# Hi parts from ScalarE, lo parts from VectorE, in the output and up projections of a two-layer transformer

## The chip, the cores and the metric

The kernel runs on one core of one Trainium2 chip. The metric is the time of one execution on the device in microseconds (us); a smaller number is better. The engines are called PE (TensorE, the matrix engine), DVE (VectorE), ACT (ScalarE), POOL (GpSimd) and SP (SyncE, which issues nearly all DMAs). Each works off its own instructions strictly in order, and waits where an operand is not there yet.

## The reference, cut to what matters

Two layers over 1024 latent tokens of width 1024, with 256 context tokens in front. Layer 0 mixes tokens by a gated MLP beside a neighbourhood attention, layer 1 by grouped-query attention. Then each layer does the same, here for the latent tokens (in layer 0 the context tokens take the same path):

```python
y = mixed @ w_out                                   # output projection, 1024 x 1024
h = h + gt_m * rms_norm(y, g_post_m)
f = modulate(h, g_pre_f, sh_f, sc_f) @ w_up         # up projection, 1024 x 5632
f = conv3(f); a, g = split(f)
h = h + gt_f * rms_norm((silu(g) * a) @ w_down, g_post_f)
```

All of it is float32.

## The kernel before

A float32 product is made of three faster matmuls. `split` (L113) cuts an operand into a hi part, which is a cast to the format fp32r, and a lo part, which is the operand less its hi part. PE then adds up hi x hi, hi x lo and lo x hi. So each operand costs one CAST and one TENSOR_TENSOR, and `split` is told on which engine each is done: "s" for ACT, "v" for DVE, "p" for POOL. Weights come in by `wload` and `part`, always with the hi part (`whi`) on ACT and the lo part (`wlo`) on DVE.

`mlp()` is the function that runs for each layer from the output projection on. The **output projection** has three groups of token tiles: half A of the latent tokens, in layer 0 the context tokens (C), and half B. Each group is multiplied first with one half of the weight's columns and then with the other. The token operands of B and C (`opB`, `opC`) are read back from memory, eight tiles each of 128x512 (B) or 128x256 (C), and are split in `out_load` (L405) while A is being multiplied. In the trace these tiles are called `xb` (parts) and `xd` (what was read); the matmuls are those of `gemm_tok`, L319 to L321, which write `by`.

The **up projection** forms a 1024x1024 by 1024x5632 product by a scheme of seven products in place of eight (after Strassen and Winograd). The activations are cut into blocks, and the seven moving operands are B11, B21, T2, T1, T3, B22 and T4; T1 to T4 are differences of blocks, formed by the subtractions at L938. Four 128x512 tiles make one operand. In the trace the parts of T2 are `xb24` to `xb31`, those of T1 `xb0` to `xb7`, those of T3 `xb8` to `xb15`, and those of B22 and T4 are `xd` tiles, with `xe` for the very last lo part. For each of the 22 column blocks `run` takes two weight blocks, forms two pairs of weight sums on POOL (`sw`, L460 and L461, then L463 and L464), splits them, multiplies (`product`, L500 to L502) and adds the seven results together (`z`, L479 on DVE and POOL). PE's order in a column begins with B11, B21, then T2, T1, T3, B22, T4. POOL's second pair of sums goes into the same tile as the first, so it waits until the first pair's `wlo` on DVE has been formed.

In the kernel before, `out_load` casts on DVE, and the lo parts of even tiles come from DVE, those of odd tiles from POOL. T2 is split on DVE altogether. T1, T3, B22 and T4 are cast on DVE, with lo parts again from DVE (even) and POOL (odd). A framework sets the order of the instructions of each engine beforehand, by a model of their durations and of what they depend on; the order in which the program creates them decides only between those that could run at once. `issue_after(x)`, which the change uses, makes it place instructions behind the instruction x.

Of the kernel before, what the change touches and what calls it, by code (L numbers as in the profile page):

```python
# [9 lines left out]
F32 = mybir.dt.float32  # L10
F32R = mybir.dt.float32r
AF = mybir.ActivationFunctionType
ALU = mybir.AluOpType
# [5 lines left out]
T = 1024  # L19
C = 256  # L20
# [8 lines left out]
HF = 512  # L29
# [26 lines left out]
class Net:  # L56
# [55 lines left out]

    def split(self, hi, lo, src, hi_eng="s", lo_eng="v"):  # L113
        nc = self.nc
        if hi_eng == "s":
            nc.scalar.copy(hi, src)  # L116
        else:
            nc.vector.tensor_copy(hi, src)  # L118
        if lo_eng == "p":
            nc.gpsimd.tensor_tensor(lo, src, hi.bitcast(F32), op=ALU.subtract)  # L120
        else:
            nc.vector.tensor_tensor(lo, src, hi.bitcast(F32), op=ALU.subtract)  # L122

    def wload(self, src, shape):
        raw = self.t(self.wp, [P, 1024], "wraw", 3)
# [279 lines left out]
    def out_load(self, xm, k, yT, c0, n, raw, eng):  # L405
        nc = self.nc
        nc.sync.dma_start(raw[:, :n], yT[k][:, c0:c0 + n])
        if eng == "sp":
            self.split(xm[0][k][:, :n], xm[1][k][:, :n], raw[:, :n], "s", "p")
        elif eng == "pp":  # L410
            nc.gpsimd.tensor_scalar(xm[0][k][:, :n], raw[:, :n], 1.0, 1.0, op0=ALU.mult, op1=ALU.mult)
            nc.gpsimd.tensor_tensor(xm[1][k][:, :n], raw[:, :n], xm[0][k][:, :n].bitcast(F32), op=ALU.subtract)
        else:
            self.split(xm[0][k][:, :n], xm[1][k][:, :n], raw[:, :n], "v", eng)
# [461 lines left out]
    def mlp(self, xa, opA, l, ctx, yT, w_out, src, mid, dst, ahead=None, after=None):  # L876


        nc, tc = self.nc, self.tc
# [5 lines left out]
        with ExitStack() as e0:  # L885
# [3 lines left out]
            with self.banks(out=4, turn=2):  # L889
              with self.banks(junk=1, tmp=1):  # L890
                with ExitStack() as e1:
                  xb2 = pool("xd", e1)
                  E = lambda dt=F32: self.t(xb2, [P, HF], "xd", 16, dt)
                  with ExitStack() as e2:
# [10 lines left out]
                      opB = [[B(8 * i + k) for k in range(KD)] for i in range(2)]  # L905
                      opC = None
                      for k in range(KD):
                          self.out_load(opB, k, yT, HF, HF, E(), "p" if k % 2 else "v")
                      if ctx:
                          opC = [halves(B(16 + k)) for k in range(KD)]  # L910
                          opC = [[x[:, i] for x in opC] for i in range(2)]
                          for k in range(KD):
                              self.out_load(opC, k, yT, T, C, E(), "p" if k % 2 else "v")

                      def ops(t):
                          o = opC if t >= 8 else opB if t >= 4 else opA
# [3 lines left out]
                      op = self.out_proj(ops, w_out, [[0, 1, 2, 3]] + ([[8, 9]] if ctx else []) + [[4, 5, 6, 7]], gates, src, mid)  # L920
# [15 lines left out]
                      st = {v: [E() for _ in range(4)] for v in ("T1", "T3", "B22", "T4")}  # L936
# [4 lines left out]
                      X = {v: ([A() for _ in range(4)], [A() for _ in range(4)]) for v in ("B11", "B21")}  # L941
# [12 lines left out]
                      for c, hs in zip((0, 256), pairs):  # L954
                          self.turned(hs, mod, 0, lambda j: f("B22" if j >= 4 else "T3", j % 4, c))
                          for k in range(4):
                              T1, T3, B22, T4 = (f(v, k, c) for v in ("T1", "T3", "B22", "T4"))
                              x = self.tmp()
                              sub(nc.vector, T1, T3, T1)
                              sub(nc.vector, x, B22, T1)  # L960
                              sub(nc.gpsimd, T3, B22, T3)
                              sub(nc.vector, T4, x, T4)
                              self.split(T2[0][k][:, c:c + 256], T2[1][k][:, c:c + 256], x, "v", "v")
                      assert next(op, None) is None


# [9 lines left out]
                  with ExitStack() as e3:  # L976
                      up.append(pool("up", e3))

                      free = [lambda i=i: B(i) for i in range(16)] + [lambda: E(F32R)] * 15 + [lambda: self.t(up[0], [P, HF], "xe", 1, F32R)]
                      for v in ("T1", "T3", "B22", "T4"):  # L980
                          X[v] = [], []
                          for k in range(4):
                              for i in range(2):
                                  X[v][i].append(free.pop(0)())
                              self.split(X[v][0][k], X[v][1][k], st[v][k], "v", "p" if k % 2 else "v")
                      run(X, Xc, load_w, load_h)
              with self.banks(junk=2):
                sink = ahead(A, B, self.mod_cols(1, 0)) if ahead else None
# [763 lines left out]
    def run(self):  # L1752
        nc, a, tc, es = self.nc, self.a, self.tc, self.es
        dram = lambda tag, n: [self.t(self.dr, [P, D], f"{tag}{t}") for t in range(n)]
        hM, hF, hG = dram("hM", NT), dram("hF", NT), dram("hG", 8)
        self.yT = [self.t(self.dr, [P, S], f"yT{i}") for i in range(KD)]
        self.yT1 = [self.t(self.dr, [P, T], f"yU{i}") for i in range(KD)]
        at = lambda lst: (lambda t: lst[t])
        stream = lambda t: 1 if t >= 8 else 0
        seg0 = lambda src, c: [(src(t), P, stream(t), (t - 5 * c) * P) for t in range(5 * c, 5 * c + 5)]  # L1760
        self.constants()
        with self.work(5), self.banks(one=3, two=2, ada=1):
            self.ldq = nc.sync
            mod, ready = self.even_start(seg0(self.h0, 0))
            self.constants2()
            self.es_na = ExitStack()
            self.even_in(mod, ready, seg0(self.h0, 1))
        xs = ExitStack()
        xp, xm0 = self.even_attn(xs)

        def mixer_in(B):
            self.odd_in(xs, B)

        self.mlp(xp, xm0, 0, True, self.yT, a["w_out_ab"][0], self.h0, at(hM), at(hF),
                 self.odd_ahead, mixer_in)
        xs = ExitStack()
        xp, xm0 = self.odd_attn(xs)
        with xs:
            self.mlp(xp, xm0, 1, False, self.yT1, a["w_out_c"][0], at(hF), at(hG), lambda t: self.out[0, t * P:(t + 1) * P, :])
# [69 lines left out]
```

## Time and profile before

| | |
|---|---|
| runs of the kernel before | 2975.86, 2983.38, 2984.0 us, median 2983.38 |
| profiled execution | 2972.55 us, its span 2970.8 |
| mean granted clock of PE, share of full speed | 0.979 |
| busy: PE, DVE, ACT, POOL | 2844.2, 2115.3, 1326.0, 1611.4 us |

The profile is of one execution, the profiled one. A row of the timeline gives the start, the duration, the engine, the line of the kernel, the operation with its output and input tiles, and in square brackets the idle time just before it with the operation that ended it. In the tables of waits the same idle times are summed by what ended them. The granted clock of PE has two levels, 1.2 and 2.4 GHz, given as a share of the upper one: a row at 0.5 is a stretch at the lower one.

### The profile page before, as it was taken

What the parts mean: (1) busy time and instruction counts of PE and PEld (TensorE: products, weight loads), DVE (VectorE), ACT (ScalarE), POOL (GpSimd) and SP (SyncE); (2) the same over time, 40 slices, a digit from 0 to 9 for tenths busy, and PEclk for the clock granted to TensorE, in tenths of its full rate; (3) what the DMA queues carried; (4) which work ended last, traced back from release to release, by engine and by line L of the source; (5) the groups of instructions that cost most, each with busy time, mean ns of one, the idle gap of its engine ahead of it and who ended that gap; (6) DMA issues with size and microseconds to landing.
All of it is one profiled execution on the core that took longest, in us unless ns stands there. A gap on an engine that the chain in (4) does not pass through costs nothing. (4 is left out here: it accounts for less than half of the span.)

```text
span 2970.8 us, 42877 instructions
## 1 busy us (share of the span) xinstructions
PE 2844.2 (96%) x15699; PEld 2265.2 (76%) x15699; DVE 2115.3 (71%) x2598; ACT 1326.0 (45%) x2351; POOL 1611.4 (54%) x1500
## 2 busy tenths in 40 slices
PE   8999989998999999999989989999998999999997
PEld 6878967776888888877769966666676788887785
DVE  4441255569766776698897668788757888877998
ACT  4321056373333343444456555555545444444443
POOL 2232277446333333265766778889955644442766
PEclk9999999999999999999999989999998999999998
DMA  8377773453323323463244462222252222225542
GB/s 311 119 226 231 233 259 106 159 196 109 112 98 119 125 79 117 165 204 119 80 139 141 140 193 97 100 100 100 89 195 78 85 85 79 85 79 194 164 142 85
DMA packets 234163, 411.28 MB, mean 138 GB/s; under 512 B 28240, under 2 KB 132688, under 8 KB 226016
## 3 DMA queue, kind: packets, MB, share of 16 engines
q1 hardware_dynamic: 211248, 392.99, 39.3%
q10 hardware_dynamic: 22704, 15.55, 1.7%
q8 instruction: 124, 2.03, 0.3%
q14 instruction: 87, 0.71, 0.1%
HBM read 303.54 MB, written 104.92 MB: 137 GB/s over the span
## 5 line engine op out<-in xcount | busy, mean ns | idle before, releaser
L463 POOL TENSOR_TENSOR sw<-wraw,wraw 128x512 f32<-128x512 f32 x44 | 61.7, 1403 | 465.4 <-DVE wlo L122 465.4
L1668 POOL TENSOR_TENSOR part<-part,pT 128x512 f32<-128x512 f32 x192 | 271.3, 1413 | 13.4
L122 DVE TENSOR_TENSOR wlo<-wraw,whi 128x1024 fp32r<-128x1024 f32 (+1 forms) x160 | 217.2, 1363 | 83.5 <-ACT whi L116 83.3
L1624 DVE TENSOR_REDUCE ng<-b 128x1 f32<-128x1280 f32 x128 | 190.9, 1491 | 80.8 <-PE b L1623 80.6
L116 ACT CAST whi<-wraw 128x1024 fp32r<-128x1024 f32 (+1 forms) x160 | 157.9, 990 | 194.5 <-PE b L310 105.1
L116 ACT CAST whi<-sw 128x1024 fp32r<-128x1024 f32 x88 | 92.3, 1049 | 334.5 <-PE by L501 252.8
L1645 ACT ACTIVATE pT<-b 128x512 f32<-128x512 f32 x320 | 170.5, 603 | 145.7 <-PE b L1644 129.4
L500 PE MATMUL by<-xb,whi 128*128 128x512 f32 x528 | 212.6, 403 | 6.5 <-DVE xb L118 3.3
L479 DVE TENSOR_TENSOR z<-by,z 128x512 f32<-128x512 f32 x176 | 120.8, 687 | 134.4 <-POOL z L479 85.8
L502 PE MATMUL by<-xb,wlo 128*128 128x512 f32 x528 | 210.9, 400 | 5.0 <-DVE wlo L122 5.0
L501 PE MATMUL by<-xb,whi 128*128 128x512 f32 x528 | 211.2, 400 | 2.0 <-DVE xb L122 2.0
L116 ACT CAST xb<-xb 128x512 fp32r<-128x512 f32 (+2 forms) x184 | 103.2, 567 | 186.7 <-PE by L873 63.3
L122 DVE TENSOR_TENSOR xb<-xb,xb 128x512 fp32r<-128x512 f32 (+2 forms) x184 | 168.6, 933 | 25.2 <-ACT xb L116 24.6
L615 POOL TENSOR_TENSOR ts<-ts 128x512 f32<-128x512 f32 x88 | 116.7, 1336 | 127.2 <-DMA ts<-in_w_down_dram 125.1
L122 DVE TENSOR_TENSOR wlo<-sw,whi 128x1024 fp32r<-128x1024 f32 x88 | 127.9, 1454 | 67.2 <-ACT whi L116 66.4
L735 POOL TENSOR_TENSOR y<-y,wraw 128x512 f32<-128x512 f32 x72 | 115.4, 1623 | 85.5 <-DVE wraw L735 54.3
L1656 PE MATMUL by<-pT,Vs 128*64 128x256 f32 x1280 | 150.7, 382 | 0.0
L500 PE MATMUL by<-xm,whi 128*128 128x512 f32 x352 | 141.9, 403 | 8.4 <-DVE z L479 4.5
L501 PE MATMUL by<-xm,whi 128*128 128x512 f32 x352 | 141.0, 401 | 0.0
L502 PE MATMUL by<-xm,wlo 128*128 128x512 f32 x352 | 140.5, 400 | 0.0
L500 PE MATMUL by<-xd,whi 128*128 128x512 f32 x352 | 139.5, 396 | 1.0 <-DVE xd L118 1.0
L502 PE MATMUL by<-xd,wlo 128*128 128x512 f32 x352 | 138.7, 394 | 0.0
(310 smaller groups left out, 9021.2 us busy)
## 6 DMA issues: line engine op xcount, KB each, us to landing
wraw<-in_w_up_t_dram SPq DMA_DIRECT2D x89, 512.0 KB
awr<-in_w_ada_dram SPq DMA_DIRECT2D x44, 1024.0 KB
ts<-in_w_down_dram SPq DMA_DIRECT2D x44, 512.0 KB
tD<-ts SPq DMA_DIRECT2D x22, 1024.0 KB
xm<-tD SPq DMA_DIRECT2D x88, 256.0 KB
hid<-o SPq DMA_DIRECT2D x43, 512.0 KB
xm<-in_w_down_dram SPq DMA_DIRECT2D x66, 256.0 KB
xb<-hid SPq DMA_DIRECT2D x66, 256.0 KB
```

The costliest lines, as they stand in the source:

```text
L116: nc.scalar.copy(hi, src)
L122: nc.vector.tensor_tensor(lo, src, hi.bitcast(F32), op=ALU.subtract)
L479: add = lambda o, x, y, e=V: e.tensor_tensor(o, x, y, op=ALU.add)
L500: nc.tensor.matmul(o, W[0][:, k, :], hi[k], start=(k == 0), stop=False)
L501: nc.tensor.matmul(o, W[0][:, k, :], lo[k], start=False, stop=False)
L502: nc.tensor.matmul(o, W[1][:, k, :], hi[k], start=False, stop=(k == 3))
L615: sub = lambda o, x, y: nc.gpsimd.tensor_tensor(o, x, y, op=ALU.subtract)
L735: add = lambda o, x, y, e=V: e.tensor_tensor(o, x, y, op=ALU.add)
L1624: nc.vector.tensor_reduce(b["ng"][:, h:h + 1], ps[:, :S], axis=AX.X, op=ALU.max, negate=True)
L1645: nc.scalar.activation(b["pT"][:, k], ps, AF.Exp)
L1656: nc.tensor.matmul(out(b["po"][:, :256], i), self.KV[b["g"]][2][:, k], two(b["pT"][:, k], i), start=(k == 0), stop=(k == NT - 1))
L1668: nc.gpsimd.tensor_tensor(x, x if k > 1 else b["pT"][:, 0], b["pT"][:, k], op=ALU.add)
```

## The change

`split` returns its two instructions, and the engines of several of its calls change:

- `out_load` for B and, in layer 0, for C: the hi part comes from ACT, and every lo part from DVE ("sv").
- T2: the hi parts of the second 256 columns (`c` is 256) come from ACT, those of the first stay on DVE; lo parts stay on DVE.
- T1, T3, B22, T4: the hi parts come from ACT; lo parts stay where they were. All these instructions are placed behind the two of T2's last split (`ends`).

```diff
@@ -112,14 +112,9 @@
 
     def split(self, hi, lo, src, hi_eng="s", lo_eng="v"):
         nc = self.nc
-        if hi_eng == "s":
-            nc.scalar.copy(hi, src)
-        else:
-            nc.vector.tensor_copy(hi, src)
-        if lo_eng == "p":
-            nc.gpsimd.tensor_tensor(lo, src, hi.bitcast(F32), op=ALU.subtract)
-        else:
-            nc.vector.tensor_tensor(lo, src, hi.bitcast(F32), op=ALU.subtract)
+        x = nc.scalar.copy(hi, src) if hi_eng == "s" else nc.vector.tensor_copy(hi, src)
+        y = (nc.gpsimd if lo_eng == "p" else nc.vector).tensor_tensor(lo, src, hi.bitcast(F32), op=ALU.subtract)
+        return x, y
 
     def wload(self, src, shape):
         raw = self.t(self.wp, [P, 1024], "wraw", 3)
@@ -405,8 +400,8 @@
     def out_load(self, xm, k, yT, c0, n, raw, eng):
         nc = self.nc
         nc.sync.dma_start(raw[:, :n], yT[k][:, c0:c0 + n])
-        if eng == "sp":
-            self.split(xm[0][k][:, :n], xm[1][k][:, :n], raw[:, :n], "s", "p")
+        if eng in ("sp", "sv"):
+            self.split(xm[0][k][:, :n], xm[1][k][:, :n], raw[:, :n], "s", eng[1])
         elif eng == "pp":
             nc.gpsimd.tensor_scalar(xm[0][k][:, :n], raw[:, :n], 1.0, 1.0, op0=ALU.mult, op1=ALU.mult)
             nc.gpsimd.tensor_tensor(xm[1][k][:, :n], raw[:, :n], xm[0][k][:, :n].bitcast(F32), op=ALU.subtract)
@@ -905,12 +900,12 @@
                       opB = [[B(8 * i + k) for k in range(KD)] for i in range(2)]
                       opC = None
                       for k in range(KD):
-                          self.out_load(opB, k, yT, HF, HF, E(), "p" if k % 2 else "v")
+                          self.out_load(opB, k, yT, HF, HF, E(), "sv")
                       if ctx:
                           opC = [halves(B(16 + k)) for k in range(KD)]
                           opC = [[x[:, i] for x in opC] for i in range(2)]
                           for k in range(KD):
-                              self.out_load(opC, k, yT, T, C, E(), "p" if k % 2 else "v")
+                              self.out_load(opC, k, yT, T, C, E(), "sv")
 
                       def ops(t):
                           o = opC if t >= 8 else opB if t >= 4 else opA
@@ -960,7 +955,7 @@
                               sub(nc.vector, x, B22, T1)
                               sub(nc.gpsimd, T3, B22, T3)
                               sub(nc.vector, T4, x, T4)
-                              self.split(T2[0][k][:, c:c + 256], T2[1][k][:, c:c + 256], x, "v", "v")
+                              ends = self.split(T2[0][k][:, c:c + 256], T2[1][k][:, c:c + 256], x, "s" if c else "v", "v")
                       assert next(op, None) is None
 
 
@@ -977,12 +972,14 @@
                       up.append(pool("up", e3))
 
                       free = [lambda i=i: B(i) for i in range(16)] + [lambda: E(F32R)] * 15 + [lambda: self.t(up[0], [P, HF], "xe", 1, F32R)]
+
                       for v in ("T1", "T3", "B22", "T4"):
                           X[v] = [], []
                           for k in range(4):
                               for i in range(2):
                                   X[v][i].append(free.pop(0)())
-                              self.split(X[v][0][k], X[v][1][k], st[v][k], "v", "p" if k % 2 else "v")
+                              with tc.issue_after(ends[0].ins), tc.issue_after(ends[1].ins):
+                                  self.split(X[v][0][k], X[v][1][k], st[v][k], "s", "p" if k % 2 else "v")
                       run(X, Xc, load_w, load_h)
               with self.banks(junk=2):
                 sink = ahead(A, B, self.mod_cols(1, 0)) if ahead else None
```

In the whole program DVE has 2509 rows in place of 2561, ACT 2192 in place of 2128 and POOL 1284 in place of 1296; PE and SP have the same numbers. In lists of the order below, the lines of the kernel after the change are smaller by 5 or 6 (the subtraction of `split` is L122 before and L116 after on DVE, its cast L118 before on DVE and L115 after on both engines; L938 is L933, L479 is L474).

On DVE in layer 0's output projection, before the change, ahead of the lo part `wlo_1437` of the first weight tile of A's second column half:

```order
L118 CAST xb18_1377_5779<-xd_1385_5793 128x256
L118 CAST xb19_1378_5780<-xd_1386_5797 128x256
L122 TENSOR_TENSOR xb18_1377_5779<-xd_1385_5793,xb18_1377_5779 128x256
L118 CAST xb20_1379_5781<-xd_1387_5801 128x256
L118 CAST xb21_1380_5782<-xd_1388_5805 128x256
L122 TENSOR_TENSOR xb20_1379_5781<-xd_1387_5801,xb20_1379_5781 128x256
L118 CAST xb22_1381_5783<-xd_1389_5809 128x256
L118 CAST xb23_1382_5784<-xd_1390_5813 128x256
L122 TENSOR_TENSOR wlo_1437_5979<-wraw_1435_5977,whi_1436_5978 128x1024
```

and after it:

```order
L116 TENSOR_TENSOR xb16_1375_5777<-xd_1383_5785,xb16_1375_5777 128x256
L116 TENSOR_TENSOR xb17_1376_5778<-xd_1384_5789,xb17_1376_5778 128x256
L116 TENSOR_TENSOR xb18_1377_5779<-xd_1385_5793,xb18_1377_5779 128x256
L116 TENSOR_TENSOR xb19_1378_5780<-xd_1386_5797,xb19_1378_5780 128x256
L116 TENSOR_TENSOR xb20_1379_5781<-xd_1387_5801,xb20_1379_5781 128x256
L116 TENSOR_TENSOR wlo_1437_5979<-wraw_1435_5977,whi_1436_5978 128x1024
L116 TENSOR_TENSOR xb21_1380_5782<-xd_1388_5805,xb21_1380_5782 128x256
```

The casts are gone from this engine, every subtraction is on it, and the weight's lo part stands ahead of the last three of them.

On DVE at the start of layer 0's up projection, before the change; `z_1706` adds the second product of the first column, and `xb0` to `xb8` are parts of T1 and T3:

```order
L118 CAST xb2_1669_7041<-xd_1392_5818 128x512
L938 TENSOR_TENSOR xd_1394_5820<-xd_1398_5824,xd_1394_5820 128x256
L122 TENSOR_TENSOR xb1_1668_7038<-xd_1391_5817,xb0_1667_7037 128x512
L938 TENSOR_TENSOR xd_1406_5832<-bm_1660_6966,xd_1406_5832 128x256
L118 CAST xb27_1571_6546<-bm_1660_6966 128x256
L118 CAST xb4_1671_7045<-xd_1393_5819 128x512
L118 CAST xb8_1675_7053<-xd_1395_5821 128x512
L118 CAST xb6_1673_7049<-xd_1394_5820 128x512
L479 TENSOR_TENSOR z_1706_7127<-by_1707_7129,z_1706_7127 128x512
```

and after it, the rows up to the same addition, then those at the end of T2:

```order
L933 TENSOR_TENSOR xd_1406_5832<-bm_1660_6966,xd_1406_5832 128x256
L115 CAST xb27_1571_6546<-bm_1660_6966 128x256
L116 TENSOR_TENSOR xb31_1575_6550<-bm_1660_6966,xb27_1571_6546 128x256
L933 TENSOR_TENSOR bm_1665_7007<-xd_1399_5825,xd_1391_5817 128x256
L474 TENSOR_TENSOR z_1706_7127<-by_1707_7129,z_1706_7127 128x512
```

```order
L933 TENSOR_TENSOR bm_1666_7020<-xd_1402_5828,xd_1394_5820 128x256
L933 TENSOR_TENSOR xd_1406_5832<-bm_1666_7020,xd_1406_5832 128x256
L116 TENSOR_TENSOR wlo_1711_7175<-sw_1702_7107,whi_1710_7174 128x1024
L116 TENSOR_TENSOR xb31_1575_6550<-bm_1666_7020,xb27_1571_6546 128x256
L116 TENSOR_TENSOR xb1_1668_7038<-xd_1391_5817,xb0_1667_7037 128x512
L116 TENSOR_TENSOR xb5_1672_7046<-xd_1393_5819,xb4_1671_7045 128x512
```

The casts of T1 and T3 are gone from the rows ahead of `z_1706`, and the first subtraction of T1 (`xb1`) now stands behind the last one of T2 (`xb31`) and behind the second weight's lo part `wlo_1711`.

On DVE at the start of layer 1's up projection, before the change, from an addition to the weight's lo part `wlo_4472`, which T2 and T1 are multiplied with:

```order
L118 CAST xd_4450_21941<-xd_4232_20961 128x512
L479 TENSOR_TENSOR z_4479_22036<-by_4480_22038,z_4479_22036 128x512
L122 TENSOR_TENSOR xb9_4443_21926<-xd_4228_20957,xb8_4442_21925 128x512
L118 CAST xb10_4444_21929<-xd_4229_20958 128x512
L122 TENSOR_TENSOR xb28_4340_21421<-bm_4432_21879,xb24_4336_21417 128x256
L118 CAST xb12_4446_21933<-xd_4230_20959 128x512
L118 CAST xb14_4448_21937<-xd_4231_20960 128x512
L122 TENSOR_TENSOR xd_4451_21942<-xd_4232_20961,xd_4450_21941 128x512
L938 TENSOR_TENSOR bm_4432_21879<-xd_4233_20962,xd_4225_20954 128x256
L122 TENSOR_TENSOR xb13_4447_21934<-xd_4230_20959,xb12_4446_21933 128x512
L479 TENSOR_TENSOR z_4484_22069<-by_4485_22071,z_4484_22069 128x512
L122 TENSOR_TENSOR wlo_4472_21985<-sw_4470_21981,whi_4471_21984 128x1024
```

and after it:

```order
L474 TENSOR_TENSOR z_4474_22001<-by_4475_22003,z_4474_22001 128x512
L474 TENSOR_TENSOR z_4479_22036<-by_4480_22038,z_4479_22036 128x512
L116 TENSOR_TENSOR xb28_4340_21421<-bm_4432_21879,xb24_4336_21417 128x256
L933 TENSOR_TENSOR bm_4432_21879<-xd_4233_20962,xd_4225_20954 128x256
L933 TENSOR_TENSOR xd_4237_20966<-bm_4432_21879,xd_4237_20966 128x256
L116 TENSOR_TENSOR xb29_4341_21422<-bm_4432_21879,xb25_4337_21418 128x256
L933 TENSOR_TENSOR bm_4433_21892<-xd_4234_20963,xd_4226_20955 128x256
L933 TENSOR_TENSOR xd_4238_20967<-bm_4433_21892,xd_4238_20967 128x256
L116 TENSOR_TENSOR wlo_4472_21985<-sw_4470_21981,whi_4471_21984 128x1024
```

Ahead of `wlo_4472` there are now only differences (L933) and subtractions of T2.

## Rows read from the trace of the kernel before

**Rows 1.** The page, busy time of each engine.

```profile
PE 2844.2 (96%) x15699; PEld 2265.2 (76%) x15699; DVE 2115.3 (71%) x2598; ACT 1326.0 (45%) x2351; POOL 1611.4 (54%) x1500
```

**Rows 2.** Waits of PE in 557:570, 680:720, 2186:2203, 2290:2325 (total, times, longest).

```profile
PE by L320 <- DVE wlo L122: 5.4, 1, 5.4
...
PE by L500 <- DVE z L479: 4.5, 1, 4.5
PE by L500 <- DVE xb L118: 3.3, 1, 3.3
...
PE by L320 <- DVE wlo L122: 4.7, 3, 2.7
...
PE by L502 <- DVE wlo L122: 5.0, 2, 4.4
PE by L501 <- DVE xb L122: 1.8, 1, 1.8
PE by L500 <- DVE xd L118: 1.0, 2, 0.7
```

**Rows 3.** Windows behind the waits: length, PE busy, PEclk, DMA share, GB/s.

```profile
563.10:568.00 4.90, 4.90 (x12) 0.51 0.52 135
685.70:692.00 6.30, 6.24 (x20) 0.60 0.00 0
695.30:701.70 6.40, 6.35 (x21) 0.56 0.62 223
2199.80:2203.00 3.20, 3.13 (x8) 0.52 0.52 161
...
2300.80:2305.20 4.40, 4.37 (x10) 0.50 0.13 20
```

**Rows 4.** Timeline of DVE at the start of layer 0's up projection.

```profile
676.22 0.42 DVE L118 CAST xb<-xd 128x512 fp32r<-128x512 f32 x1
...
678.84 0.96 DVE L118 CAST xb<-xd 128x512 fp32r<-128x512 f32 x1
...
680.05 1.77 DVE L122 TENSOR_TENSOR xb<-xd,xb 128x512 fp32r<-128x512 f32 x1
...
682.41 2.69 DVE L118 CAST xb<-xd 128x512 fp32r<-128x512 f32 x3
685.03 0.68 DVE L479 TENSOR_TENSOR z<-by,z 128x512 f32<-128x512 f32 x1
...
686.74 0.68 DVE L122 TENSOR_TENSOR xb<-xd,xb 128x512 fp32r<-128x512 f32 x1
```

**Rows 5.** Casts on DVE by shape, in 676:720 and in 544:564.

```profile
L118 DVE CAST xd<-xd 128x512 fp32r<-128x512 f32 x8 | 7.3, 916 | 0.0
...
L118 DVE CAST xb<-xd 128x512 fp32r<-128x512 f32 x8 | 5.4, 690 | 0.0
...
L118 DVE CAST xb<-xd 128x512 fp32r<-128x512 f32 x8 | 6.4, 817 | 3.0 <-DMA xd<-yT 3.0
L118 DVE CAST xb<-xd 128x256 fp32r<-128x256 f32 x8 | 5.7, 753 | 0.0
```

**Rows 6.** The page, casts of `split` that ACT does already.

```profile
L116 ACT CAST xb<-xb 128x512 fp32r<-128x512 f32 (+2 forms) x184 | 103.2, 567 | 186.7 <-PE by L873 63.3
```

**Rows 7.** Timeline of DVE in layer 0's output projection.

```profile
561.83 1.21 DVE L122 TENSOR_TENSOR wlo<-wraw,whi 128x1024 fp32r<-128x1024 f32 x1
```

**Rows 8.** Timeline of ACT in layer 0's output projection.

```profile
552.81 1.06 ACT L116 CAST whi<-wraw 128x1024 fp32r<-128x1024 f32 x1
...
567.56 1.05 ACT L116 CAST whi<-wraw 128x1024 fp32r<-128x1024 f32 x1 [9.21 <-DMA wraw<-in_w_out_ab_dram]
```

**Rows 9.** Timeline of POOL at the start of layer 0's up projection.

```profile
694.62 1.27 POOL L463 TENSOR_TENSOR sw<-wraw,wraw 128x512 f32<-128x512 f32 x1 [2.69 <-DVE wlo L122]
...
710.95 1.30 POOL L120 TENSOR_TENSOR xe<-xd,xd 128x512 fp32r<-128x512 f32 x1 [1.76 <-DVE xd L118]
```

**Rows 10.** Timeline of PE, the next column's third product (T3) in layer 0.

```profile
720.13 0.39 PE L500 MATMUL by<-xb,whi 128*128 128x512 f32 x1
```

## The prediction

> **What bounds the kernel now.** I read the page's busy times first: the matrix engine (PE) is busy 96% of the span, VectorE (DVE) 71%, ScalarE (ACT) 45% and GpSimd (POOL) 54% [rows 1]. So a gain can only come from places where PE stands still or runs at its slow clock, and the diff touches four: the end of each layer's output projection, where the groups B and C of its token operand are split, and the start of each layer's up projection, where T2, T1, T3, B22 and T4 are split. The second view is the waits of PE in just these stretches: 5.4 us in layer 0's output projection, 4.5 and 3.3 at its up projection's start, 4.7 (three waits) in layer 1's output projection, and 5.0, 1.8 and 1.0 at its up projection's start [rows 2]. All are waits for DVE, 25.7 us together. The third view is the granted clock right behind these waits: about half (1.2 GHz in place of 2.4) in five stretches [rows 3]. Length times what is missing from 1 gives 4.9 x 0.49 = 2.4, 6.3 x 0.40 = 2.5, 6.4 x 0.44 = 2.8, 3.2 x 0.48 = 1.5 and 4.4 x 0.50 = 2.2, together 11.4. What can come back at most is therefore 25.7 + 11.4 = 37 us, in shares of A 7.8 (layer 0, output), B 13.1 (layer 0, up), C 6.2 (layer 1, output) and D 10.0 (layer 1, up).
>
> **What leaves and what comes.** DVE loses 64 casts: 16 in layer 0's output projection, 8 in layer 1's, and 20 in each up projection. It takes over from POOL the subtraction of 8 lo parts in layer 0 and 4 in layer 1. ACT gets all 64 casts, at 0.567 us for a 128x512 by the mean of those it does already [rows 6]: at most 48 x 0.57 + 16 x 0.57 = 36 us, on an engine that is busy 45% and stands idle for 9.21 us in one piece in layer 0's output projection [rows 8]. I cost ACT's part at nothing as long as the casts' inputs are there; the case where they are not is the third rival. PE and the queue of DMA issues keep the same instructions.
>
> A cast on DVE is dear here because it often stands beside POOL's work: 0.42 us alone, 0.96 and 3 x 0.90 a little later [rows 4]. In the stretch at layer 0's up projection the 16 casts of T1 to T4 take 7.3 + 5.4 = 12.7 us, and in its output projection the 16 take 6.4 + 5.7 = 12.1 [rows 5].
>
> **A, layer 0's output projection.** PE waits for the lo part of one weight tile, 561.83 to 563.04 on DVE [rows 7]; its hi part was done at 552.81 + 1.06 = 553.87 on ACT [rows 8]. Between them DVE only worked off the casts and subtractions of B and C. In the new order this subtraction stands behind 13 subtractions and none of the casts. Of them 8 are 128x512 at 0.68 us (a lo part at 686.74 [rows 4]) and 5 are half as long, some 0.4, from 544.4 on at the earliest: 7.4 us of work. So what decides is ACT: 13 casts, three copies of y and the weight's own cast lie ahead, some 13 x 0.5 + 2.5 + 1.05 = 10 us from 544.4, which is 554.5, and the lo part follows at about 556. PE stopped at 563.04 - 5.4 = 557.6. The wait goes, with its stretch of slow clock: 7.8. What is late next is the weight behind it, which came by DMA after 9.21 us of idle on ACT [rows 8]; its tile is freed earlier by the same 7 us, but may be held by loads already queued. Bounds 4 to 7.8, taken 7.
>
> **B, layer 0's up projection.** The wait of 4.5 is for one addition, z, on DVE at 685.03 [rows 4]. Ahead of it five of the removed casts took 0.42 + 0.96 + 2.69 and a lo part of T1 1.77, 5.8 us together [rows 4]; in the new order a lo part of T2 and one difference have moved ahead (about 0.8). So z starts at about 680 to 681 and PE, free at 685.7 - 4.5 = 681.2, goes on at once. The wait of 3.3 for a cast of T1 or T2 changes its nature: T2 now has to be whole first, and its last subtraction stands behind a weight's lo part that needs two weight sums on POOL. Those sums were held up in the old order by 2.69 us until another lo part on DVE was done at 694.5 [rows 9]; that one comes about 6 us earlier. I expect T2's last matmul at about 692.5 and a wait of 1 to 3 inside it. From there POOL sets the pace: eight lo parts at 1.30, and among them four weight sums and an addition at 1.3 to 1.4, 10.4 + 6.9 = 17.3 us, from about 691 on, when the first cast of T1 is through. Its last lo part, that of T4, then ends near 708.5, and was done at 710.95 + 1.30 = 712.25 [rows 9]. In the old order PE still had 8 us of work behind that, and reached the next column's third product at 720.13 [rows 10]; now T2 and T1 of the next column are placed ahead of the end of T4, and PE's own work, 13.1 us of loss taken away, would be through at 707. So this point comes at about 709 to 710 and B gives 10, bounds 3 (POOL's end alone) to 13.1.
>
> **C, layer 1's output projection.** Eight casts leave DVE; at the mean of the eight of the same shape in layer 0, 817 ns [rows 5], that is 6.5 us in front of three lo parts that PE awaits for 4.7 together. ACT must have the weights' hi parts in time and waits there for the loads of the operand; bounds 1 to 6.2, taken 5.
>
> **D, layer 1's up projection.** The weight's lo part that PE awaits longest (4.4 of the 5.0 [rows 2]) stands 12 rows earlier against the two z additions, with no cast of T1 to T4 ahead. If its 16 casts cost as in layer 0 that is 12.7 us off the queue, more than the 10.0 at stake; but POOL's seventeen microseconds follow here too, and PE's waits for the activations before (which the change does not touch) stay. Bounds 2 to 10, taken 8.
>
> **Sum.** 7 + 10 + 5 + 8 = 30. I take off 5 for waits that appear where none were: 2 in A for the weights' DMA, 3 in B and D for the slow clock behind the new waits in T2. That leaves 25. The profiled execution took 2972.55 (span 2970.8 and 1.75 around it), so 2947.5, which is 0.84% less. It was 10.8 below the median of the runs shown, 2983.38; the same share off the median is 2958, which is my forecast. Its own range is 2945 to 2967.
>
> **Rivals.** First, POOL and DVE go on stopping one another. For it: a lo part took 1.77 us on DVE at 680.05 and 0.68 at 686.74, POOL being at work in the first case [rows 4]; the subtractions stay, and are now dense on both engines. Then a removed cast saves only its 0.42, some 8 us for 20, and POOL's 17.3 us stretch by a fifth (1.30 towards the 1.77 that DVE shows), so T4 comes as late as before. B and D give 4 each and A and C, where POOL has no lo parts left, 10: 18 less 3, so 2968. Against it: in A and C the same change takes POOL's reads away.
>
> The Trainium skill, SBUF — State Buffer, section Who interferes with whom, says that a VectorE instruction with two inputs in SBUF contends with a GpSimd instruction that reads SBUF, and that whoever is first has the shared ports for its whole length. By that rule the lock moves from the cast to the subtraction behind it, and the sum would be the rival's; the two durations of the lo part agree with it.
>
> Second, what is won is given back: the column loop behind each start has its own pace, set by weights and DVE, and the earlier PE merely waits there. For it: DVE has 71% busy over the span and was the releaser of all these waits. Against it: PE is at 96%, so it rarely waits later. A third of the 25 would be left: 2975 to 2980.
>
> Third, slower: ACT works strictly in its order. In the new order every cast of T1 to T4 stands behind the hi part of a weight that needs POOL's sums, and T2 is first in PE's order, so PE has no T1 or T3 to run beside it. If those sums come as late as before (694.62 + 2 x 1.35, so 697.3 [rows 9]), ACT's row of casts begins at 698.5 and, with 0.6 for the first of them, POOL's 17.3 us end at 716.4: 4 later than 712.25. PE has nothing else to run in these 4, and loses about as much again at half clock. With T2's own wait of 3 that is 11 in each layer's start, 22, against 6 from A and C: 16 slower, 3000. It decides when the lo part awaited by the sums starts later than about 692 in place of 687. Against it: nothing but subtractions is left ahead of it on DVE.
>
> That the change does not do what it says is excluded by the order: T2's last subtraction stands ahead of T1's first on DVE.
>
> **How the numbers follow.** The forecast has 0.50, the first rival 0.22, the second 0.16, the third 0.12. About 0.3%, 9 us, is what a measurement can tell from no change. Faster by more: 0.50 + 0.20 of the first and a little of the second, 0.72; within it 0.17, nearly all the second; slower 0.11. The range reaches from 2942, where nearly all that is at stake comes back, to 2984, beyond the second rival, and leaves out most of the third and a little below.
>
> **What would show it.** Right: the waits of 5.4 and 4.5 gone and no slow clock behind them; z at about 681; T4's last lo part on POOL near 708; the next column's third product near 710 in place of 720. Wrong: waits of PE inside T2 of more than 4 us, subtractions on DVE of 1.3 and more in a row, or POOL's last lo part of T4 at 712 or later; or later waits in the column loops that grow by as much as these shrink.

## The result and the profile after

The changed kernel takes 2956.86 us in the median; the ratio to the kernel before is 0.9917, with a 95% interval of 0.9903 to 0.9931. Of the five runs of each kernel one took far longer (5615.45 us before, 11655.27 after) and is left out of the ratio; the other four have medians of 2979.62 and 2954.86, 24.8 apart. The forecast was 2958 and a factor of 0.9916. The profiled execution of the changed kernel has 2956.86 us too (span 2955.0), against 2972.55 of the one before; only 15.7 apart, where the medians of the four are 24.8 apart. Why is told below.

The page after, busy time of each engine, answers to [rows 1]:

```profile
PE 2837.8 (96%) x15699; PEld 2259.0 (76%) x15699; DVE 2094.4 (71%) x2546; ACT 1355.5 (46%) x2415; POOL 1597.0 (54%) x1488
```

DVE lost 20.9 us of busy time and ACT gained 29.5, within the 36 allowed.

The waits of PE after, in the same four stretches, answer to [rows 2]. Both output projections (548:566 and 2180:2200) have none. These are the larger ones at the start of layer 0's up projection (670:712), then of layer 1's (2279:2312); the smaller ones add up to 1.3:

```profile
PE by L496 <- DVE xd L116: 1.5, 1, 1.5
PE by L495 <- ACT xb L115: 1.0, 2, 0.6
...
PE by L497 <- DVE wlo L116: 2.3, 1, 2.3
PE by L496 <- POOL xe L116: 1.3, 1, 1.3
```

The four lines hold 6.1 us in place of the 25.7 of before. Windows of PE after (length, PE busy, clock, DMA share, GB/s) answer to [rows 3]:

```profile
560.00:564.00 4.00, 4.00 (x19) 1.00 0.62 225
690.00:695.00 5.00, 5.00 (x26) 1.00 0.42 125
2291.00:2295.60 4.60, 4.33 (x10) 0.50 0.34 114
...
2190.00:2200.00 10.00, 10.00 (x44) 1.00 0.62 234
```

Of the five stretches at the slow clock one is left, behind the wait of 2.3 in layer 1 (4.60 x 0.50 = 2.3 lost). A new one has come outside these places: at layer 0's hand-over, which is what I call the way from the output to the up projection, PE runs from 624 to 628 at 0.57 (1.7 lost), where the trace before has 1.00 for the same matmuls (635 to 639).

To place the gain I compare the start of the same matmul in both traces. The difference (after less before) is -3.2 us when PE works on the last of A's first column half in layer 0's output projection, -11.0 when it is at the context tokens there, -8.7 shortly ahead of the start of layer 0's up projection, -16.7 in the last columns of layer 0's up projection, -16.6 in its down projection, -5.6 ahead of layer 1's output projection's loads, -12.5 at the end of that stretch, -11.5 at the first product behind the transposes, -17.0 in the columns after, and -15.8 at the end of the span. So the four places gave A 7.8, B 8.0, C 6.9 and D 5.5, together 28.2; at the two hand-overs 2.3 and 1.0 were lost again. 24.9 are the change's. The rest lies outside what was changed: 3.2 came before the first changed instruction, 1.2 were lost between layer 1's columns and the end, and 11.0 were lost in the attention of layer 1, which the change leaves as it was. There the waits of PE for L1621 (L1624 before) are these in the trace before, in the trace after, and in a second execution of the changed kernel:

```profile
PE b L1623 <- DVE ng L1624: 9.1, 8, 2.1
```

```profile
PE b L1620 <- DVE ng L1621: 15.3, 15, 3.2
```

```profile
PE b L1620 <- DVE ng L1621: 8.7, 6, 3.2
```

These waits account for 6.2 of the 11.0. The second execution lost 1.6 us in that whole stretch in place of 11.0, and ended with a span of 2945.7. In the twelve traces of the experiments, the second execution among them, this stretch lost between -0.6 and 5.1 against the trace before, so the 11.0 is the exception. One execution of this kernel can differ from the next by some nine microseconds in the attention, and two profiles should be compared stage by stage.

### The profile page after: what moved, and what is told of

The parts are those of the page before. It is cut to its first block, busy times and chain, and to the rows that moved or that the text cites. A ratio compares the mean times of both kernels' runs of the same rounds, so it can differ in the third digit from the quotient of the medians.

```text
span 2955.0 us, 42885 instructions
## 1 busy us (share of the span) xinstructions
PE 2837.8 (96%) x15699; PEld 2259.0 (76%) x15699; DVE 2094.4 (71%) x2546; ACT 1355.5 (46%) x2415; POOL 1597.0 (54%) x1488
## 5 line engine op out<-in xcount | busy, mean ns | idle before, releaser
L116 DVE TENSOR_TENSOR wlo<-wraw,whi 128x1024 fp32r<-128x1024 f32 (+1 forms) x160 | 212.2, 1332 | 84.0 <-ACT whi L115 84.0
L1621 DVE TENSOR_REDUCE ng<-b 128x1 f32<-128x1280 f32 x128 | 190.8, 1490 | 81.5 <-PE b L1620 81.2
L115 ACT CAST whi<-wraw 128x1024 fp32r<-128x1024 f32 (+1 forms) x160 | 157.5, 990 | 181.9 <-PE b L305 104.9
L115 ACT CAST whi<-sw 128x1024 fp32r<-128x1024 f32 x88 | 92.2, 1048 | 268.1 <-PE by L496 237.4
L474 DVE TENSOR_TENSOR z<-by,z 128x512 f32<-128x512 f32 x176 | 120.7, 686 | 132.1 <-POOL z L474 85.7
L115 ACT CAST xb<-xb 128x512 fp32r<-128x512 f32 (+2 forms) x184 | 103.4, 567 | 180.9 <-PE by L868 63.0
L116 DVE TENSOR_TENSOR xb<-xb,xb 128x512 fp32r<-128x512 f32 (+2 forms) x184 | 165.7, 915 | 26.2 <-ACT xb L115 25.7
L116 DVE TENSOR_TENSOR wlo<-sw,whi 128x1024 fp32r<-128x1024 f32 x88 | 131.9, 1499 | 61.9 <-ACT whi L115 61.5
L513 DVE SCALAR_TENSOR_TENSOR o<-z,cw,o 128x1023 f32<-128x1023 f32 x88 | 140.3, 1597 | 2.8 <-ACT o L512 2.6
```

The source lines that it names most:

```text
L115: x = nc.scalar.copy(hi, src) if hi_eng == "s" else nc.vector.tensor_copy(hi, src)
L116: y = (nc.gpsimd if lo_eng == "p" else nc.vector).tensor_tensor(lo, src, hi.bitcast(F32), op=ALU.subtract)
L474: add = lambda o, x, y, e=V: e.tensor_tensor(o, x, y, op=ALU.add)
L513: V.scalar_tensor_tensor(o[:, 1:], z[:, :n - 1], cw(0), o[:, 1:], op0=ALU.mult, op1=ALU.add)
L1621: nc.vector.tensor_reduce(b["ng"][:, h:h + 1], ps[:, :S], axis=AX.X, op=ALU.max, negate=True)
```

## The experiments

For each run, besides its ratio, I give what each place gained or lost in its trace against the trace before, by the start of the same matmuls: A is from the end of A's first column half to the last products ahead of layer 0's up projection's start, B from there to the last columns, C and D likewise in layer 1. PE's wait for the copy of the first product into z, at the head of the up projection, is counted in B and D. Hand-overs are counted in A and C, which is why the changed kernel has -5.5 there and not -7.8. The values move by some 0.5 with the matmul that is taken as the border.

| run | A | B | C | D | ratio to before (95%) |
|---|---|---|---|---|---|
| changed kernel | -5.5 | -8.0 | -5.9 | -5.5 | 0.9917 (0.9903 to 0.9931) |
| e1_out_only | -5.5 | -0.4 | -5.2 | -0.6 | 0.9958 (0.9943 to 0.9973) |
| e2_up_only | +0.4 | -7.3 | +0.7 | -5.7 | 0.9966 (0.9954 to 0.9978) |
| e3_no_order | -7.6 | -3.3 | -6.0 | -7.7 | 0.9932 (0.9920 to 0.9944) |
| e4_order_only | +1.3 | +2.2 | +0.6 | +2.3 | 1.0020 (1.0010 to 1.0029) |
| e5_out_sp | -6.7 | -6.9 | -5.6 | -5.9 | 0.9913 (0.9901 to 0.9925) |
| e6_up_lo_dve | -5.6 | -8.3 | -5.5 | -6.9 | 0.9897 (0.9884 to 0.9910) |
| e7_out_all_dve | -8.3 | -0.9 | -6.0 | +3.5 | 0.9962 (0.9950 to 0.9975) |
| e8_t2_act | -7.4 | -2.4 | -5.1 | -2.2 | 0.9929 (0.9917 to 0.9941) |
| e9_order_l0 | -7.8 | -7.4 | -5.7 | -6.9 | 0.9921 (0.9906 to 0.9936) |
| e10_order_l0_lo_dve | -8.0 | -8.2 | -5.7 | -7.7 | 0.9893 (0.9878 to 0.9909) |
| e11_after_again | -7.3 | -7.0 | -5.8 | -5.7 | 0.9910 (0.9894 to 0.9926) |
| e12_out_dve_up_new | -8.2 | -7.2 | -7.0 | -1.9 | 0.9929 (0.9910 to 0.9948) |

**The output projection alone (e1_out_only).** The splits of the up projection are as in the kernel before:

```diff
-self.split(T2[0][k][:, c:c + 256], T2[1][k][:, c:c + 256], x, "s" if c else "v", "v")
+self.split(T2[0][k][:, c:c + 256], T2[1][k][:, c:c + 256], x, "v", "v")
-with tc.issue_after(ends[0].ins), tc.issue_after(ends[1].ins):
-    self.split(X[v][0][k], X[v][1][k], st[v][k], "s", "p" if k % 2 else "v")
+self.split(X[v][0][k], X[v][1][k], st[v][k], "v", "p" if k % 2 else "v")
```

> Only the change to out_load: hi parts of B and C on ScalarE, all their lo parts on VectorE; the up projection as before. Theory 1 (each place gives back the waits of PE that it had, and the places add up): the waits of 5.4 in layer 0's and of 4.7 in layer 1's output projection go with their slow clock, some 14 us, of which 2 to 4 are lost again at the hand-over to the up projection; 10 to 13 us less than before, ratio 0.9957 to 0.9967. Rival (the output projection's gain is swallowed by what follows, and the up projection alone makes the result): at most 4 us less, ratio above 0.9985.

Measured: 2958.02 us, ratio 0.9958, 12 us. In its trace PE has no wait in layer 0's output projection and one of 0.3 in layer 1's, and the up projections' starts are as before (waits of 4.3 and 2.7 us in layer 0 for DVE, 5.5 in layer 1). The theory of waits held.

**The up projection alone (e2_up_only).** The loads of the output projection are as in the kernel before:

```diff
-self.out_load(opB, k, yT, HF, HF, E(), "sv")
+self.out_load(opB, k, yT, HF, HF, E(), "p" if k % 2 else "v")
-self.out_load(opC, k, yT, T, C, E(), "sv")
+self.out_load(opC, k, yT, T, C, E(), "p" if k % 2 else "v")
```

> Only the change to the splits of T2, T1, T3, B22 and T4, with their order; out_load as before. Theory 1: the gain at the starts of the up projections stays, 8 in layer 0 and 6 in layer 1, together 12 to 15 us less than before, ratio 0.995 to 0.996, and the two out-projection waits of 5.4 and 4.7 are as before. Rival (this gain exists only because the output projection comes earlier or frees ScalarE): less than 8 us.

Measured: 2960.45 us, ratio 0.9966, 10 us, a little short of the 12 to 15; its trace has 7.3 + 5.7 = 13.0 at B and D, within them. The waits for the weights' lo parts in the output projections are there as before (4.5 and 4.3). The two halves add up: 1 - 0.9958 + 1 - 0.9966 = 0.0076, with 0.0083 for the whole.

**The casts without the order (e3_no_order).**

```diff
-with tc.issue_after(ends[0].ins), tc.issue_after(ends[1].ins):
+if True:
```

> The changed kernel without the two issue_after: casts of T1, T3, B22 and T4 may go ahead of T2 on ScalarE. Theory 1 (what counts is that the casts leave VectorE): within 3 us of the changed kernel, ratio 0.991 to 0.993. Rival (T2 at the head does the work): the casts of T1 stand ahead of the weights' hi parts and of z's copies on ScalarE, waits of PE of 3 to 5 us come back in each up projection, 5 to 10 us slower than the changed kernel, ratio 0.994 to 0.995.

Measured: 0.9932 (0.9920 to 0.9944), between the two; the interval takes in the ends of both. The order does one thing in layer 0 and another in layer 1: B has -3.3 in place of -8.0, D -7.7 in place of -5.5. In layer 0 the copy of the first product into z stands on ACT behind three casts of T1 and T3 (it runs at 672.61, they from 669.23 on), and PE waits for it at the head of the stretch (waits of PE, 668:722):

```profile
PE by L495 <- ACT z L524: 4.2, 1, 4.2
PE by L496 <- DVE xb L116: 1.4, 2, 0.9
PE by L495 <- ACT xb L115: 1.3, 1, 1.3
```

That wait is 1.6 with the order. In layer 1 it is 3.3 without it (waits of PE, 2270:2330), as the rival had it, but there the wait of 2.3 for the second weight's lo part shrinks to two of 0.8, and none is left for `xe`:

```profile
PE by L495 <- ACT z L524: 3.3, 1, 3.3
PE by L497 <- DVE wlo L116: 1.7, 2, 0.8
```

**The order without the casts (e4_order_only).**

```diff
-self.split(T2[0][k][:, c:c + 256], T2[1][k][:, c:c + 256], x, "s" if c else "v", "v")
+self.split(T2[0][k][:, c:c + 256], T2[1][k][:, c:c + 256], x, "v", "v")
-    self.split(X[v][0][k], X[v][1][k], st[v][k], "s", "p" if k % 2 else "v")
+    self.split(X[v][0][k], X[v][1][k], st[v][k], "v", "p" if k % 2 else "v")
```

(with out_load as before)

> The kernel before with T2 at the head of the order (issue_after), all casts where they were before. Theory 1: VectorE still has its 20 casts per layer, now in one row behind T2; the wait for z (4.5) goes, but T1 to T4 come later and PE has nothing beside T2: between 4 us less and 4 us more than before, ratio 0.9987 to 1.0013. Rival (the order does the work): 8 us or more less than before, ratio under 0.9973.

Measured: 1.0020 (1.0010 to 1.0029), some 6 us slower, a little beyond the expected range and clearly not the rival's. B and D each lose over 2. DVE, still with all its casts, is busy 9.9 of 10 us from 690 to 710, and PE waits behind T2: in layer 1 3.6 us for `xb` lo parts and 3.1 for `xd` casts. In these runs the order pays only with the casts elsewhere.

**Lo parts on POOL again in the output projection (e5_out_sp).**

```diff
-self.out_load(opB, k, yT, HF, HF, E(), "sv")
+self.out_load(opB, k, yT, HF, HF, E(), "sp" if k % 2 else "sv")
```

(likewise for C)

> The changed kernel, but in out_load the lo parts of odd tiles stay on GpSimd as before; only the casts move. Theory 1 (the casts off VectorE are what counts): no wait of PE over 1 us for a weight's lo part in the output projections, within 3 us of the changed kernel, ratio 0.991 to 0.993. Rival (the lock between VectorE and GpSimd is what counts): VectorE's lo parts beside GpSimd's take 1.3 to 1.8 in place of 0.7, the weights' lo parts come late again, waits of 2 to 4 us in each of the two, 4 to 8 us slower than the changed kernel.

Measured: 0.9913, as the changed kernel; one wait of 0.5 in layer 0. The lock of the rival is there (the weights' lo parts take 1.98 in the mean in 540:564, against 1.24 in the changed kernel), but of the waits of 2 to 4 that it was to bring only the 0.5 came: the weights' lo parts are nearly in time even so.

**Everything on DVE in the output projection, POOL's lo parts out of it (e7_out_all_dve).**

```diff
-self.out_load(opB, k, yT, HF, HF, E(), "p" if k % 2 else "v")
+self.out_load(opB, k, yT, HF, HF, E(), "v")
```

(likewise for C; the rest is the kernel before)

> The kernel before with all of out_load on VectorE, casts and lo parts; nothing on GpSimd or ScalarE. Lock theory: without GpSimd's reads a cast takes 0.42 in place of 0.82, so VectorE's work ahead of the weights' lo parts shrinks by 3 to 6 us although it has 8 lo parts more: 3 to 7 us less than before, ratio 0.9977 to 0.999. Theory 1 without the lock: the work ahead of the weight's lo part grows by 4 us, waits of 8 to 9 in layer 0: 3 to 6 us more than before, ratio 1.001 to 1.002.

Measured: 0.9962, 11 us: more than the lock theory expected, and the opposite of what theory 1 without the lock did. DVE by shape in 540:564, first the casts, then the lo parts, against 817 and 753 ns per cast in [rows 5]:

```profile
L118 DVE CAST xb<-xd 128x512 fp32r<-128x512 f32 x8 | 3.2, 422 | 2.1 <-DMA xd<-yT 2.1
...
L118 DVE CAST xb<-xd 128x256 fp32r<-128x256 f32 x8 | 2.0, 285 | 0.0
...
L122 DVE TENSOR_TENSOR xb<-xd,xb 128x512 fp32r<-128x512 f32 x8 | 5.4, 685 | 0.0
L122 DVE TENSOR_TENSOR xb<-xd,xb 128x256 fp32r<-128x256 f32 x8 | 3.2, 419 | 0.0
```

32 instructions take 13.8 us where 24 took 12.1 + 6.9 = 19.0 beside POOL. PE has no wait left in layer 0's output projection, and one of 2.3 in layer 1's. The price is POOL's: its four products with the gate, beside this row, take 17.1 us, against 5.8 in the kernel before, one row of four:

```profile
547.12 17.13 POOL L350 TENSOR_TENSOR y<-y,gate 128x512 f32<-128x512 f32 x4 [14.62 <-DMA xd<-yT]
```

**The same with the changed up projection (e12_out_dve_up_new).** The edit is that of the run before, on the changed kernel.

> The up projection as changed, out_load all on VectorE (casts and lo parts, nothing on ScalarE or GpSimd). Lock theory (in the output projection it is enough that either the casts leave VectorE or the lo parts leave GpSimd): as fast as the changed kernel, within 3 us. Rival (the casts have to leave VectorE, and the gain of the run with out_load alone on VectorE came from elsewhere): the waits for weights' lo parts in the output projections return, 5 us or more slower than the changed kernel.

Measured: 2958.37 against 2953.69 for the changed kernel beside it, ratio 0.9929 (0.9910 to 0.9948) against 0.9910: 4.7 slower, between the two expectations; the two intervals overlap. There is no wait in layer 0's output projection, and one of 2.7 in layer 1's. So in layer 0 either removal is enough. In layer 1 a part of the wait stays when the casts do, but C as a whole is no worse for it (-7.0 against -5.8 beside it, and -6.0 in e7_out_all_dve). What is lost is D, -1.9 against -5.7. Its waits there (2262:2300) are other ones than those of the changed kernel:

```profile
PE by L495 <- ACT xb L115: 3.0, 3, 2.1
PE by L496 <- POOL xb L116: 2.4, 1, 2.4
```

T2's last lo part starts at 2276.57 on DVE, against 2273.38 in the changed kernel beside it, now behind the second weight's lo part, and POOL's first lo part of T1, which is placed behind T2, at 2280.50 against 2274.46. Why the order came out so was not tested.

**All lo parts of T1 to T4 on DVE (e6_up_lo_dve).**

```diff
-    self.split(X[v][0][k], X[v][1][k], st[v][k], "s", "p" if k % 2 else "v")
+    self.split(X[v][0][k], X[v][1][k], st[v][k], "s", "v")
```

> The changed kernel with all lo parts of T1, T3, B22 and T4 on VectorE, none on GpSimd. Theory 1 with GpSimd as the pace of the up projection's start: its last lo part ended at 703.0 there after eight of 1.3 to 2.3 us; without them the next column's products come 2 to 4 us earlier in each layer, 4 to 8 us less than the changed kernel, ratio 0.9888 to 0.9903. Rival (VectorE becomes the pace): 16 lo parts at 0.7 to 1.7 stand ahead of the weights' lo parts there, waits of PE for wlo of 2 to 5 us, 3 to 8 us slower than the changed kernel.

Measured: 2950.23 us, ratio 0.9897, the number expected of POOL as the pace. The 15 lo parts of T1 to T4 on DVE take 8.7 + 5.0 us in 672:712:

```profile
L116 DVE TENSOR_TENSOR xd<-xd,xd 128x512 fp32r<-128x512 f32 x7 | 8.7, 1283 | 0.1
L116 DVE TENSOR_TENSOR xb<-xd,xb 128x512 fp32r<-128x512 f32 x8 | 5.0, 683 | 0.0
```

In the changed kernel the same stretch has 7.0 + 5.3 on DVE for eight, and on POOL 7.0 + 5.2 for seven more:

```profile
L116 DVE TENSOR_TENSOR xd<-xd,xd 128x512 fp32r<-128x512 f32 x4 | 7.0, 1764 | 1.8 <-POOL xb L116 1.2 <-POOL xd L116 0.6
...
L116 DVE TENSOR_TENSOR xb<-xd,xb 128x512 fp32r<-128x512 f32 x4 | 5.3, 1359 | 0.0
```

```profile
L116 POOL TENSOR_TENSOR xb<-xd,xb 128x512 fp32r<-128x512 f32 x4 | 7.0, 1747 | 2.6 <-ACT xb L115 2.6
L116 POOL TENSOR_TENSOR xd<-xd,xd 128x512 fp32r<-128x512 f32 x3 | 5.2, 1771 | 0.0
```

So 15 on one engine cost DVE 1.4 us more than eight beside POOL. The trace shows only 1.7 us of gain at B and D together (0.3 in layer 0), less than the 6 of the ratios, or the 4 against the 0.9910 that the changed kernel had when it was measured again. So the trace does not show POOL as the pace in layer 0.

**T2's first half on ACT too (e8_t2_act).**

```diff
-self.split(T2[0][k][:, c:c + 256], T2[1][k][:, c:c + 256], x, "s" if c else "v", "v")
+self.split(T2[0][k][:, c:c + 256], T2[1][k][:, c:c + 256], x, "s", "v")
```

> The changed kernel with the hi parts of T2's first 256 columns on ScalarE too. Theory 1: VectorE was not what PE waited for there, so nothing changes: within 1.5 us of the changed kernel, ratio 0.9912 to 0.9922. Rival (ScalarE becomes late, its activations stand between VectorE's difference and its lo part, and each of four round trips adds 0.3): 1.5 to 4 us slower in place of it.

Measured: 0.9929, 3.6 us slower than the changed kernel, as the rival had it. The intervals of the two overlap, but the trace is clear: B and D fall to -2.4 and -2.2, from -8.0 and -5.5. DVE forms a difference in one of a few buffers, waits for the cast on ACT, subtracts and goes on:

```profile
685.95 0.42 DVE L933 TENSOR_TENSOR xd<-bm,xd 128x256 f32<-128x256 f32 x1
686.81 0.42 DVE L116 TENSOR_TENSOR xb<-bm,xb 128x256 fp32r<-128x256 f32 x1 [0.44 <-ACT xb L115]
```

and ACT works in order: one of these casts, at 678.65, stands behind a copy of z that waits 3.5 us for PE, and behind a weight's hi part. T2's last lo part starts at 688.6 in place of 680.7 in the changed kernel; 2 of these 8 us were there at the start of the stretch.

**Order in layer 0 alone, then also all lo parts on DVE, with the changed kernel beside them (e9_order_l0, e10_order_l0_lo_dve, e11_after_again).**

```diff
-with tc.issue_after(ends[0].ins), tc.issue_after(ends[1].ins):
+with (tc.issue_after(ends[0].ins) if ctx else ExitStack()), (tc.issue_after(ends[1].ins) if ctx else ExitStack()):
```

> The changed kernel with issue_after in layer 0 alone; in layer 1 the casts may go ahead of T2. Theory (read off the run without any order, where the start of layer 0's up projection came out about 5 us worse and that of layer 1 about 4 us better than in the changed kernel): the two add up, layer 0 as changed and layer 1 as without order, 3 to 5 us less than the changed kernel beside it. Rival (the 4 in layer 1 was chance of one execution or hung on layer 0's end): within 1.5 us of it.

> As the run before, with the lo parts of T1, T3, B22 and T4 all on VectorE. Theory (GpSimd's lo parts of 1.7 us set the pace behind T2, and without them VectorE's take 0.7): another 1 to 3 us less than the run before, 4 to 8 less than the changed kernel. Rival (in layer 1 without order VectorE has these lo parts ahead of T2's differences): slower than the run before by 2 to 5 us.

> The changed kernel once more, on the same chip as the three beside it. All theories: ratio to the kernel before between 0.9903 and 0.9931, the interval it had.

Measured: 2955.12 (0.9921), 2947.70 (0.9893) and 2953.69 us (0.9910). The first is not faster than the changed kernel: the rival. D has -6.9 in place of -5.7, 1.2 better and not the 4 that I had read off, because the wait for the copy of z (3.3 in place of 1.6) belongs to it; the medians show nothing of that. The second is 6.0 below the changed kernel, 7.4 below the first; all its five times are from 2943.26 to 2949.80, those of the changed kernel from 2947.51 to 2956.20. With e6_up_lo_dve it makes two runs in which POOL without lo parts of T1 to T4 is 0.13 to 0.24% better than the changed kernel, by whichever of its two ratios one goes; here the order in layer 1 differs as well. It is the fastest version that I have, by a difference that the intervals do not separate.

## Why the prediction was right, step by step

**What bounds.** Right: the gain lies in the four places, and each half of the change gives back its own waits and nothing else (e1, e2).

**A, 7 predicted, 7.8 measured.** The weight's lo part starts at 552.32:

```profile
552.32 1.22 DVE L116 TENSOR_TENSOR wlo<-wraw,whi 128x1024 fp32r<-128x1024 f32 x1
```

On the clock of the trace before, 3.2 later, that is 555.5, and its end 556.7; predicted was about 556. The DMA that I took 2 us off for did not bind. In its place 2.3 went at the hand-over. PE waits 2.0 for an activation of `h` there (618:632 after) in place of 1.2 (629:641 before), and runs the stretch behind it at the slow clock:

```profile
PE b L371 <- ACT h L359: 2.0, 1, 2.0
```

```profile
PE b L376 <- ACT h L364: 1.2, 1, 1.2
```

**B, 10 predicted, 8.0 measured.** The addition z was at 670.02, which is 678.8 on the clock before (8.7 later); predicted was 680 to 681. Both waits of 4.5 and 3.3 are gone, T2 waits 1.0 inside (predicted 1 to 3). The term that was mis-sized is POOL's row. I took 1.30 for a lo part, from a single row [rows 9], 17.3 us in all and an end at 708.5; the eight in the trace before had taken 1.28 to 2.14. After the change a lo part took 1.75 and the last one 2.27:

```profile
700.77 2.27 POOL L116 TENSOR_TENSOR xe<-xd,xd 128x512 fp32r<-128x512 f32 x1
```

Its end, 703.04, is 711.8 on the clock before, hardly ahead of the 712.25 there. So on POOL the first rival was right, and one of the signs that I had named for being wrong came: DVE's subtractions in a row took 1.36 (`xb`) and 1.76 (`xd`) in the mean, over 1.3. It cost little because PE did not wait for POOL in layer 0: the next column's T2 and T1, 24 matmuls of 0.23, stand ahead of it and filled the time. What it did cost is 1.5 for a lo part of `xd` on DVE. The next column's third product starts at 703.56, which is 712.3 on the clock before and not 709 to 710, so it comes 7.8 earlier and not 10. Of the 5.1 that are missing from the 13.1, PE's waits in the stretch (1.5, 1.0 and 0.6 for a DMA) are 3.1; the other 2.0 I have not placed. Here the rule of the Trainium skill (SBUF — State Buffer, section Who interferes with whom) that I had weighed is borne out in both directions: DVE's subtractions take 1.76 beside POOL's and 0.68 without, and POOL's take 1.75 beside them. What this costs depends on whether the engine that is held up is the one that PE waits for: in e5_out_sp it was not, in the kernel before it was.

**C, 5 predicted, 6.9 measured.** All three waits went, and the slow clock with them. It is 0.7 more than all that I had counted there; these 0.7 I have not placed.

**D, 8 predicted, 5.5 measured.** The wait of 4.4 went, but one of 2.3 took its place, for the lo part of the second weight, which stands behind four lo parts of T1 and T3 on DVE:

```profile
2283.22 4.09 DVE L116 TENSOR_TENSOR xb<-xd,xb 128x512 fp32r<-128x512 f32 x3
...
2288.93 2.28 DVE L116 TENSOR_TENSOR wlo<-sw,whi 128x1024 fp32r<-128x1024 f32 x1
```

Alone these would take 3 x 0.68 and 1.21. Here POOL's row came due too: PE waits 1.3 for `xe`. With the half clock behind the first wait these are 5.9 us, of which the forecast had allowed 2 out of 10.0, besides its share of the 3 taken off for B and D. The forecast spoke of the first weight's lo part, which is in time, and not of the second's; POOL's row it had named, without a price. By this count 4.1 would be left, and 5.5 were measured, so some of the old loss was more than I had counted.

**The sum.** 28.2 less 3.3, 24.9, against 30 less 5. The over-estimates of B and D (2.0 and 2.5) are larger than the under-estimates of A and C (0.8 and 1.9), and the 5 taken off is 1.7 too much, which makes up for the rest. That 24.9 and 25 agree so closely is luck; the terms are right to within 2.5. The second rival, that the column loops give the gain back, did not come: the difference is -16.7 behind layer 0's start and -16.6 in its down projection, -17.0 behind layer 1's and -15.8 at the end. The third rival, a slow ACT, did not come, since the weight sums on POOL were done at 678.5, which is 687 on the clock before, and not at 697; e8_t2_act shows that a loss on ACT was near: four more casts of 128x256 there per layer cost 3.6 us by the ratios. The price that I gave a cast on ACT, 0.567 for 128x512, was a mean over three shapes [rows 6]; eight of 128x512 in a row take 0.53 each.

What is left open: why the ratios of the runs with all lo parts on DVE are 4 to 7 us better than the changed kernel's while their traces show 2 to 3 at B and D, and why T2 comes later in layer 1 behind an output projection that keeps its casts on DVE.

## What to carry to other kernels

When the busiest engine waits for one small instruction on another, count what stands ahead of it on that engine's queue and take that off; here the gain was the wait and the slow clock behind it, place by place, less new waits behind them, and the two halves of the change added up. If two engines hold each other up, moving the work of either away may be enough, as in layer 0's output projection, and it is worth trying the cheaper. A round trip to another engine inside a chain (difference, cast, subtraction) should be avoided where the chain is what is awaited.

## What the runs showed of the hardware

A cast of 128x512 took 0.42 us on DVE in a row of DVE without gaps (e7_out_all_dve), and 0.82 in the mean where DVE and POOL split by turns (the kernel before); a subtraction 0.68, and 1.76 beside POOL's subtractions (the changed kernel). In the first case it was POOL that was held up: its 128x512 products took 1.45 in the mean beside the casts and subtractions of before, and 4.3 beside the dense row. ACT casts 128x512 tiles at 0.53 each in a row (eight in 4.26 us), with DVE and POOL at work beside it.
